# All complex products of the S5 tables on VectorE, both parts added in one step, and priority for the q, k and v projections

## The chip, the cores and the metric
The kernel runs on one core of one Trainium2 chip. A time is the device time of one execution in microseconds (us); lower is better. The engines are called as the profile calls them: PE is TensorE, PEld its weight loads, DVE is VectorE, ACT is ScalarE, POOL is GpSimd, SP issues most DMAs.

## The reference, cut to what matters
One encoder layer over 512 tokens of width 1024 in float32: a normalised input is projected into u, q, k, v, z and gates; an S5 mixer (a diagonal complex state space, forward and backward) works on u, a gated delta rule on q, k, v; then cross-attention over a memory of 256 rows, and a mixture of 32 experts, two for each token.
```
u, q, k, v, z, beta_f, beta_b, a_f, a_b = _split_cols(h @ w_in[l])
...
lam_bar = jnp.exp(lam * step)
b_bar = ((lam_bar - 1.0) / lam)[:, :, None] * b
...
_, h = lax.associative_scan(combine, (a, bu), reverse=reverse, axis=1)
return (jnp.einsum('bsgp,gcp->bsgc', h.real, c_re.astype(F32))
        - jnp.einsum('bsgp,gcp->bsgc', h.imag, c_im.astype(F32)))
...
qkv = jax.nn.silu(_centred_depthwise_conv(jnp.concatenate([q, k, v], axis=-1), conv_w))
...
u_c = lax.linalg.triangular_solve(l_mat, v_beta, left_side=True, lower=True, unit_diagonal=True)
```

## The kernel before, in words
The S5 scan is done in blocks of eight tokens. For it `s5_params` builds tables of powers of the complex decay times b and c: for each of eight rounds gg it makes two complex products of 128 partitions x 512 elements, **pm** (powers aF times b1) and **ca** (powers aR times ct). `cmul` makes a complex product of six instructions (four multiplications, a subtraction, an addition), on VectorE or on GpSimd by the two tables CA_ENG and PM_ENG (1 is GpSimd): nine of the sixteen products on GpSimd, seven on VectorE. The tensor engine then transposes pm (L372), an ACT copy takes it to bcT, `s5_u` multiplies it with u into U (L404), and ca is multiplied with bb into the table wl (L381).

In the same stretch stand the twelve projections of q, k and v (four heads each). `gdn_in` takes one after the other: `proj` is eight matmuls 128x512 with K = 1024 (L143; each matmul leaves two records in the trace), then a depthwise convolution of four scalar_tensor_tensor instructions on VectorE (L639), SiLU on ACT, transposes on PE (L648), and a norm. `weave((qkv, 13), (s5, 9))` writes the two streams' instructions alternately. Each engine's order is fixed before the run by the scheduler of the tile framework: an instruction's place in the code is its priority, unless a priority block raises it, and the scheduler lets what it takes to be ready earlier go first.

The stages behind it, by the names that the argument uses. **The gates**: small matmuls of the gates into a bank, gc copied from it on VectorE (L579), exponentials on ACT (L580, L583), and copies (L589 to L598). **The inversion** (`gdn_inv`): four rounds, each with an outer difference on PE (L703), e on VectorE (L707), exponentials on ACT, products of k with k and q (L716, L717) and N on VectorE (L720); then a transpose NT (L731), 31 substitution steps on VectorE, transposes XT and XN (L749, L750), and small matmuls (L768 to L778). It is woven with the four z projections (32 matmuls of the L143 kind), with key and value blocks of the memory (`mem_kv`, eight matmuls 128x256 each at L143 and two transposes at L958) and with the 62 steps of the S5 recurrence on VectorE (four instructions 128x64, L414 to L417). **The chain** (`gdn_chain`): eight chunks x four heads, L834 (products with the state), L835 (r, on VectorE), L840 (a product that this text counts from 1 to 32), L851 and L854 (the new state), woven with the remaining key and value blocks. After it come the S5 output (`s5_out`, L446), the mixing, the cross-attention, and the experts, whose weights stream from HBM (L1340).

Of the kernel before, what the change touches and what calls it, by code (L numbers as in the profile page):

```python
# [9 lines left out]
F32 = mybir.dt.float32  # L10
# [4 lines left out]
AF = mybir.ActivationFunctionType  # L15
OP = mybir.AluOpType
# [15 lines left out]
P = 128  # L32
# [11 lines left out]
def weave(*streams):  # L44

    live = [[g, n, 0] for g, n in streams]
    while live:
        s = min(live, key=lambda t: (t[2] + 0.5) / t[1])
        s[2] += 1
        if next(s[0], s) is s:  # L50
            live.remove(s)


CA_ENG = (1, 1, 0, 1, 1, 1, 0, 1)
PM_ENG = (0, 0, 1, 0, 1, 0, 1, 0)


class Enc:
# [162 lines left out]
    def cmul(self, eng, pool, ore, oim, are, aim, bre, bim, shape, tag):  # L221
# [7 lines left out]
        eng.tensor_tensor(oim, aim, bre, op=OP.mult)  # L229
        eng.tensor_tensor(oim, oim, t2, op=OP.add)  # L230

    def s5_params(self):
        nc, A, tc = self.nc, self.A, self.tc
        sp = self.s5p
        v, g_ = nc.vector, nc.gpsimd
        with tc.tile_pool(name="s5t", bufs=1, side="right") as tq:
            ct = tq.tile([P, 2, 32, 16], F32, name="ct")
            dT = tq.tile([16, 32], F32, name="dT")
            aF = tq.tile([P, 2, 8, 32], F32, name="aF")
            aR = tq.tile([P, 2, 8, 32], F32, name="aR")  # L240
            bb = tq.tile([P, 2, 34, 16], F32, name="bb")
            b1 = tq.tile([P, 2, 32, 16], F32, name="b1")
            with tc.tile_pool(name="s5i", bufs=1, side="right") as tp:
                lamrow = tp.tile([32, 2, 128], F32, name="lamrow")
                for di, dn in enumerate('fb'):
# [18 lines left out]
                ps = self.ps("s5")  # L264
# [7 lines left out]
                for ri in range(2):  # L272
                    ps = self.ps("s5")
                    for b in range(4):
                        nc.tensor.transpose(ps[:, b * P:(b + 1) * P], crow[:, ri, b, :], self.ident)
                    nc.scalar.activation(ct[:, ri].rearrange("p g c -> p (g c)"), ps, AF.Copy, scale=1.0 - 2.0 * ri)

                tl = lambda s: tp.tile([P, 32], F32, name="q" + s)
                step, mg, th, r, sn, cs, t1, t2 = (tl(s) for s in ("st", "mg", "th", "r", "sn", "cs", "t1", "t2"))
# [18 lines left out]
                pw = tp.tile([P, 2, 9, 32], F32, name="pw")  # L298
# [41 lines left out]
                v.memset(bb[:, :, 32:34], 0.0)  # L340
                bg = lambda ap: ap[:, :, None].to_broadcast([P, 32, 16])
                self.cmul(v, tp, bb[:, 0, :32], bb[:, 1, :32], bg(fre), bg(fim), bt[:, 0], bt[:, 1], [32, 16], "d")
                self.cmul(v, tp, b1[:, 0], b1[:, 1], bg(pw[:, 0, 1]), bg(pw[:, 1, 1]), bb[:, 0, :32], bb[:, 1, :32], [32, 16], "d")
            yield
            with tc.tile_pool(name="s5l", bufs=1, side="right") as tl:

                dd = tl.tile([P, 8, 16], F32, name="dd")
                v.memset(dd, 0.0)
                for cg in range(4):
                    v.tensor_tensor(dd[cg * 32:cg * 32 + 16], self.ident[:16, None, :16].to_broadcast([16, 8, 16]),  # L350
                                    dT[:, cg * 8:(cg + 1) * 8, None].to_broadcast([16, 8, 16]), op=OP.mult)
                for gg in range(8):
                    gs = slice(gg, 32, 8)
                    shp = [4, 8, 16]
                    am = lambda a, ri: a[:, ri, :, gs].rearrange("p m g -> p g m")[:, :, :, None].to_broadcast([P] + shp)
                    bm = lambda b, ri: b[:, ri, gs, None, :].to_broadcast([P] + shp)

                    pm = tl.tile([P, 2] + shp, F32, name="pm", bufs=1)
                    e = PM_ENG[gg]
                    self.cmul((v, g_)[e], tl, pm[:, 0], pm[:, 1], am(aF, 0), am(aF, 1), bm(b1, 0), bm(b1, 1), shp, f"P{1 - e}")  # L360

                    ca = tl.tile([P, 2] + shp, F32, name="ca", bufs=1)
                    e = CA_ENG[gg]
                    self.cmul((v, g_)[e], tl, ca[:, 0], ca[:, 1], am(aR, 0), am(aR, 1),
                              bm(ct, 0), bm(ct, 1), shp, f"P{1 - e}")
                    nc.sync.dma_start(self.ca_scr[gg], ca.rearrange("p r g m c -> p (r g m c)"))

                    bcT = tl.tile([P, 4, 2, P], F32, name="bct", bufs=1)
                    for ri in range(2):
                        ps = self.ps("s5")  # L370
                        for cg in range(4):
                            nc.tensor.transpose(ps[:, cg * P:(cg + 1) * P], pm[:, ri, cg].rearrange("p m c -> p (m c)"), self.ident)  # L372
                        nc.scalar.activation(bcT[:, :, ri, :], ps.rearrange("p (g q) -> p g q", g=4), AF.Copy)
                    self.s5_u(gg, bcT)

                    pd = [self.ps("s5") for _ in range(2)]
                    for cg in range(4):
                        g = cg * 8 + gg
                        for di in range(2):
                            for ri in range(2):  # L380
                                nc.tensor.matmul(pd[di][cg * 32:cg * 32 + 32, :128],  # L381
                                                 bb[di * 64:(di + 1) * 64, ri, g:g + 2].rearrange("p g c -> p (g c)"),
                                                 ca[di * 64:(di + 1) * 64, ri, cg].rearrange("p m c -> p (m c)"),
                                                 start=(ri == 0), stop=(ri == 1))
                    wl = tl.tile([P, 15, 16], F32, name="wl", bufs=2)
                    pv = [t[:, :128].rearrange("p (m c) -> p m c", c=16) for t in pd]
                    v.tensor_copy(wl[:, 0:8], pv[1])
                    v.tensor_copy(wl[:, 8:15], pv[0][:, 1:8])
                    v.tensor_tensor(wl[:, 7], wl[:, 7], pv[0][:, 0], op=OP.add)
                    v.tensor_tensor(wl[:, 7], wl[:, 7], dd[:, gg], op=OP.add)  # L390
                    for cg in range(4):
                        nc.sync.dma_start(self.w_scr[:, gg * 4 + cg],
                                          wl[cg * 32:cg * 32 + 16].rearrange("p e c -> p (e c)"))
                    yield
# [1112 lines left out]
    def build(self):  # L1507
        nc, tc, ctx, A = self.nc, self.tc, self.ctx, self.A
# [18 lines left out]
        pool = lambda st, name, **kw: st.enter_context(tc.tile_pool(name=name, bufs=1, **kw))  # L1527
# [21 lines left out]
        with tc.tile_pool(name="gi", bufs=2) as gi:  # L1549
            qkv = self.gdn_in([(w, n, h) for h in range(4) for w, n in ((1, "k"), (0, "q"))] +  # L1550
                              [(2, "v", h) for h in range(4)], gi)
            s5 = self.s5_params()
            next(s5)
            for _ in u:
                pass
            weave((qkv, 13), (s5, 9))

        self.gp2 = pool(left, "gp2")
        self.gp3 = pool(left, "gp3")
# [112 lines left out]
        with tc.tile_pool(name="wk", bufs=2, **rt) as wk, tc.manual_schedule(engines={mybir.EngineType.PE, mybir.EngineType.SP}):  # L1672
# [44 lines left out]
            for b in range(4):  # L1717
                t = tile_at(b, "yb")
# [59 lines left out]
```

## Time and profile before
| what | value |
|---|---|
| runs | 889.67, 893.03, 893.8 us; median 893.03 us |
| the profiled execution | 892.26 us, span 890.5 us |
| mean granted clock of PE (1 is full) | 0.948 |
| busy: PE, PEld | 783.1 us (88%), 492.2 us (55%) |
| busy: DVE, ACT, POOL | 404.3 us (45%), 329.4 us (37%), 232.6 us (26%) |

Times are those of the slowest core; here there is one. Shares are of the whole span; the stage that the change touches is read by itself in the rows below.

### The profile page before, as it was taken

The page shows a single profiled execution, that of the slowest core. Times are in us where ns is not written, and L with a number is a line of the kernel's source. Part 1 is how long each engine was busy: PE and PEld are TensorE (multiplying, and loading weights), DVE is VectorE, ACT ScalarE, POOL GpSimd, SP SyncE. Part 2 cuts the span into 40 slices and gives each one's busy share as a digit, 9 for nine tenths or more (in the row PEclk, how much of TensorE's full clock was granted, in tenths as well). Part 3 has the DMA queues.
Part 4 walks back from the last instruction along what each step waited for, and adds up shares of the span by engine and source line. Part 5 has one row for each costly group of instructions (what it writes and reads, how often), then busy time and mean ns, then how long its engine had stood idle before and what let it go on. Part 6 is the DMA issues. An engine that isn't in the chain of part 4 may idle for free. (4 is left out here: it accounts for less than half of the span.)

```text
span 890.5 us, 12981 instructions
## 1 busy us (share of the span) xinstructions
PE 783.1 (88%) x4735; PEld 492.2 (55%) x4736; DVE 404.3 (45%) x1044; ACT 329.4 (37%) x760; POOL 232.6 (26%) x237
## 2 busy tenths in 40 slices
PE   5986998998997997899899999996698878788983
PEld 3443554555586875676688879895333333333331
DVE  4288767678899522244643554324210000000375
ACT  4242454455413235465343464333232131312204
POOL 1022857832100111205161332241311011100103
PEclk9996998999997998999999999998799999999997
DMA  7837222322663308615663714595699999999982
GB/s 206 144 91 111 74 78 74 100 76 98 225 193 104 108 24 169 116 56 172 184 224 96 260 49 159 194 406 187 248 391 412 414 411 408 395 391 410 410 350 102
DMA packets 128130, 185.17 MB, mean 208 GB/s; under 512 B 38734, under 2 KB 93006, under 8 KB 123968
## 3 DMA queue, kind: packets, MB, share of 16 engines
q1 hardware_dynamic: 122736, 172.31, 57.6%
q0 software_dynamic: 5328, 12.01, 3.6%
q8 instruction: 38, 0.62, 0.3%
q14 instruction: 28, 0.23, 0.1%
HBM read 165.50 MB, written 26.18 MB: 215 GB/s over the span
## 5 line engine op out<-in xcount | busy, mean ns | idle before, releaser
L143 PE MATMUL bank<-ht,wst 128*128 128x512 f32 x320 | 151.3, 621 | 4.2 <-ACT kd L583 2.4
L1340 PE MATMUL bank<-mw,xt 128*64 128x512 f32 x360 | 104.5, 595 | 1.5 <-DMA mw<-in_moe_w_up_dram 1.5
L143 PEld LDWEIGHTS bank<-ht,wst 128*128 128x128 f32 x320 | 60.7, 198 | 73.4 <-issue 68.3
L1344 DVE SCALAR_TENSOR_TENSOR hs<-hs,tw,bank 128x256 f32<-128x256 f32 x16 | 7.7, 480 | 168.9 <-ACT hs L1343 168.9
L1343 ACT ACTIVATE hs<-bank,tw 128x256 f32<-128x256 f32 x16 | 7.6, 474 | 155.5 <-PE bank L1340 155.5
L1380 PE MATMUL bank<-mw,hT 128*64 128x512 f32 x152 | 50.6, 660 | 16.2 <-ACT yd L1385 16.2
L1340 PEld LDWEIGHTS bank<-mw,xt 128*64 128x64 f32 x360 | 33.5, 138 | 55.6 <-issue 52.4
L143 PE MATMUL bank<-mt,wst 128*128 128x256 f32 x256 | 59.9, 393 | 0.0
L639 DVE SCALAR_TENSOR_TENSOR cv<-xp,taps,cv 128x512 f32<-128x512 f32 x48 | 50.4, 1049 | 20.8 <-ACT cv L637 19.7
L972 POOL TENSOR_TENSOR wlo<-wst,whi 128x1024 fp32r<-128x1024 f32 x16 | 38.6, 2416 | 78.7 <-ACT whi L971 78.7
L143 PEld LDWEIGHTS bank<-mt,wst 128*128 128x128 f32 x256 | 50.0, 198 | 7.7 <-issue 0.6
L1320 POOL DMA_INDIRECT xg<-t_scr,tidx x16 | 16.5, 1029 | 136.4 <-PE bank L1327 133.4
L824 POOL TENSOR_TENSOR kt<-kn,kd 64x512 f32<-64x512 f32 x14 | 14.5, 1035 | 97.6 <-PE bank L778 49.8
L1330 ACT ACTIVATE xt<-bank,gm 128x128 f32<-128x128 f32 x128 | 34.7, 382 | 8.9 <-PE bank L1327 7.8
L149 PE MATMUL bank<-wlo,oh 128*128 128x256 f32 x128 | 36.6, 289 | 0.0
L854 DVE SCALAR_TENSOR_TENSOR S<-S,egl,bank 128x128 f32<-128x128 f32 x48 | 15.5, 345 | 46.1 <-PE bank L851 46.1
L150 PE MATMUL bank<-whi,oh 128*128 128x256 f32 x128 | 35.8, 283 | 0.0
L1380 PEld LDWEIGHTS bank<-mw,hT 128*64 128x64 f32 x152 | 14.0, 148 | 38.7 <-issue 20.8
L151 PE MATMUL bank<-whi,ol 128*128 128x256 f32 x128 | 35.3, 287 | 0.0
L149 PE MATMUL bank<-mlo,mxh 128*128 128x512 f32 x64 | 25.8, 405 | 0.8 <-DVE gss L484 0.8
L903 POOL TENSOR_TENSOR mlo<-mst,mhi 128x512 fp32r<-128x512 f32 x16 | 22.0, 1393 | 14.8 <-ACT mhi L902 14.2
L150 PE MATMUL bank<-mhi,mxh 128*128 128x512 f32 x64 | 25.7, 402 | 0.0
(551 smaller groups left out, 1826.3 us busy)
## 6 DMA issues: line engine op xcount, KB each, us to landing
mw<-in_moe_w_down_dram SPq DMA_DIRECT2D x23, 1024.0 KB, 14.7
mw<-in_moe_w_gate_dram SPq DMA_DIRECT2D x45, 512.0 KB, 8.3
mw<-in_moe_w_up_dram SPq DMA_DIRECT2D x45, 512.0 KB, 13.9
wst<-in_w_in_dram SPq DMA_DIRECT2D x20, 512.0 KB, 4.5
ca_scr<-ca SPq DMA_DIRECT2D x8, 512.0 KB, 2.7
wst<-in_xa_wk_dram SPq DMA_DIRECT2D x8, 512.0 KB, 4.3
y_scr<-lhc SPq DMA_DIRECT2D x2, 2048.0 KB
wst<-in_xa_wv_dram SPq DMA_DIRECT2D x8, 512.0 KB, 4.3
```

What stands on the lines that cost most here:

```text
L143: self.nc.tensor.matmul(ps, w[:, k, :], act[:, k, :], start=(k == 0), stop=(k == 7))
L149: self.nc.tensor.matmul(ps, ah, bl, start=(first and i == 0), stop=False)
L150: self.nc.tensor.matmul(ps, ah, bh, start=False, stop=False)
L151: self.nc.tensor.matmul(ps, al, bh, start=False, stop=(last and i == n - 1))
L639: v.scalar_tensor_tensor(cv, xp[:, w:w + T], taps[:, w, m:m + 1], cv, op0=OP.mult, op1=OP.add)
L854: v.scalar_tensor_tensor(sn, S[di, h], self.egl[:, ch % 2, ch // 2, di * 4 + h:di * 4 + h + 1], p, op0=OP.mult, op1=OP.add)
L903: nc.gpsimd.tensor_tensor(lo[:, k], st, hi[:, k].bitcast(F32), op=OP.subtract)
L972: nc.gpsimd.tensor_tensor(lo, st, hi.bitcast(F32), op=OP.subtract)
L1320: self.gather = g_.indirect_dma_start(out=xg, out_offset=None, in_=self.t_scr, in_offset=bass.IndirectOffsetOnAxis(ap=self.tidx[:, q:q + 1 ...
L1330: nc.scalar.activation(xt[:, k], ps[:, (k % 4) * P:(k % 4 + 1) * P], AF.Copy, scale=self.gm[:, k:k + 1])
L1340: nc.tensor.matmul(pg[w * 64:w * 64 + 64].rearrange("p (a n) -> p a n", a=2), xt[:, k, w * 64:w * 64 + 64], un[k // 4 * 2 + w][:, :, k % 4 ...
L1380: nc.tensor.matmul(py[w * 64:w * 64 + 64], hT[:, k, w * 64:w * 64 + 64], wd[w][:, k, c], start=(k == 0), stop=(k == 1))
```

## The change
There are no tables of engines any more: all sixteen products run on VectorE, by `cprod`. It takes four multiplications of 128x512, two of them into a tile cpt that holds both parts, and one addition of 128x1024 over both parts, five instructions for six. So that the real part is an addition too, ct and b1 have a third slice with a negated imaginary part, made by one more ACT copy each. All products share the one cpt. The convolution instructions and the sizes of all else are unchanged. Besides, the generator of the q, k and v projections is wrapped in `ahead`, which raises the priority of each of its steps.
```diff
@@ -51,8 +51,15 @@
-CA_ENG = (1, 1, 0, 1, 1, 1, 0, 1)
-PM_ENG = (0, 0, 1, 0, 1, 0, 1, 0)
+def ahead(tc, g):
+
+    while True:
+        with tc.high_priority():
+            if next(g, g) is g:
+                return
+        yield
...
@@ -229,17 +236,26 @@
+    def cprod(self, pool, o, am, a, bm, b):
+
+        v = self.nc.vector
+        t = pool.tile(list(o.shape), F32, name="cpt", bufs=1)
+        for ri in range(2):
+            v.tensor_tensor(o[:, ri], am(a, 0), bm(b, 1 + ri), op=OP.mult)
+            v.tensor_tensor(t[:, ri], am(a, 1), bm(b, ri), op=OP.mult)
+        v.tensor_tensor(o, o, t, op=OP.add)
...
-            ct = tq.tile([P, 2, 32, 16], F32, name="ct")
+            ct = tq.tile([P, 3, 32, 16], F32, name="ct")
...
-            b1 = tq.tile([P, 2, 32, 16], F32, name="b1")
+            b1 = tq.tile([P, 3, 32, 16], F32, name="b1")
...
-                    nc.scalar.activation(ct[:, ri].rearrange("p g c -> p (g c)"), ps, AF.Copy, scale=1.0 - 2.0 * ri)
+                    nc.scalar.activation(ct[:, 1 + ri].rearrange("p g c -> p (g c)"), ps, AF.Copy, scale=1.0 - 2.0 * ri)
+                nc.scalar.activation(ct[:, 0].rearrange("p g c -> p (g c)"), ps, AF.Copy)
...
-                self.cmul(v, tp, b1[:, 0], b1[:, 1], bg(pw[:, 0, 1]), bg(pw[:, 1, 1]), bb[:, 0, :32], bb[:, 1, :32], [32, 16], "d")
+                self.cmul(v, tp, b1[:, 1], b1[:, 2], bg(pw[:, 0, 1]), bg(pw[:, 1, 1]), bb[:, 0, :32], bb[:, 1, :32], [32, 16], "d")
+                nc.scalar.activation(b1[:, 0], b1[:, 2], AF.Copy, scale=-1.0)
...
                     pm = tl.tile([P, 2] + shp, F32, name="pm", bufs=1)
-                    e = PM_ENG[gg]
-                    self.cmul((v, g_)[e], tl, pm[:, 0], pm[:, 1], am(aF, 0), am(aF, 1), bm(b1, 0), bm(b1, 1), shp, f"P{1 - e}")
+                    self.cprod(tl, pm, am, aF, bm, b1)
 
                     ca = tl.tile([P, 2] + shp, F32, name="ca", bufs=1)
-                    e = CA_ENG[gg]
-                    self.cmul((v, g_)[e], tl, ca[:, 0], ca[:, 1], am(aR, 0), am(aR, 1),
-                              bm(ct, 0), bm(ct, 1), shp, f"P{1 - e}")
+                    self.cprod(tl, ca, am, aR, bm, ct)
...
@@ -1553,7 +1568,7 @@
-            weave((qkv, 13), (s5, 9))
+            weave((ahead(tc, qkv), 13), (s5, 9))
```

The instruction order changes on two engines in three places that matter below. Line numbers of the changed kernel are higher than those of before by 7 at L143, by 8 to 17 in the table code and by 15 from L404 on. First, VectorE from the end of b1 (b_392) to the first pm; bank_280 holds the gates' sums, and P_637 and P_638 are scratch tiles of cmul, as cpt is of cprod. Before:
```order
L579 COPY gc<-bank_280 128x32
L228 TENSOR_TENSOR b_392<-b_392,d_560 128x512
L230 TENSOR_TENSOR b_392<-b_392,d_561 128x512
L582 TENSOR_TENSOR sdl<-bank_280,gc 128x32
L589 SCALAR_TENSOR_TENSOR sbe<-beta,egc 128x16
L594 TENSOR_SCALAR csr<-egc 64x4x4
```
and, some rows on:
```order
L225 TENSOR_TENSOR P_637<-aF,b_392 128x512
L226 TENSOR_TENSOR P_638<-aF,b_392 128x512
L593 COPY csr<-sbe 64x4x4 x2
L227 TENSOR_TENSOR pm<-aF,b_392 128x512
L229 TENSOR_TENSOR pm<-aF,b_392 128x512
L350 TENSOR_TENSOR dd<-ident,dT 16x128 x4
L228 TENSOR_TENSOR pm<-pm,P_637 128x512
L230 TENSOR_TENSOR pm<-pm,P_638 128x512
```
After:
```order
L366 MEMSET dd 128x128
L244 TENSOR_TENSOR pm<-aF,b_392 128x512 x2
L245 TENSOR_TENSOR cpt<-aF,b_392 128x512
L244 TENSOR_TENSOR ca<-aR,ct 128x512
L368 TENSOR_TENSOR dd<-ident,dT 16x128 x4
L244 TENSOR_TENSOR ca<-aR,ct 128x512
L245 TENSOR_TENSOR cpt<-aF,b_392 128x512
L594 COPY gc<-bank_280 128x32
L246 TENSOR_TENSOR pm<-pm,cpt 128x1024
L597 TENSOR_TENSOR sdl<-bank_280,gc 128x32
```
The copy of gc stands ahead of the products before; it now stands behind the four multiplications of pm and two of ca's four, with only the addition of pm behind it. The ca product of this round was on GpSimd.

Second, PE at the end of the q, k, v stage. Bank numbers 1771, 1838, 1905 and 1976 of L150 are the four z projections; L387, L396 and L419 are the transposes of pm, the products of ca and the products into U of the last two rounds; L718 is the first instruction of the inversion. After:
```order
L150 MATMUL bank_1838<-ht,wst 128x512 x3
L150 MATMUL bank_1905<-ht,wst 128x512 x6
L387 MATMUL bank_1599<-ident,pm 128x128 x4
L387 MATMUL bank_1605<-ident,pm 128x128 x4
L150 MATMUL bank_1905<-ht,wst 128x512 x2
L396 MATMUL bank_1629<-ca,bb 32x128 x8
L150 MATMUL bank_1976<-ht,wst 128x512 x3
L419 MATMUL bank_1611<-uperm,bct 64x64 x16
L396 MATMUL bank_1630<-ca,bb 32x128 x8
L718 MATMUL bank_1720<-lef,g 64x64 x8
```
All but five of the 32 z matmuls now stand ahead of the inversion's first matmul. Before, the z projections stood between the inversion's four rounds, each as in this place (L703 and L716 belong to the inversion, L143 is z):
```order
L716 MATMUL bank_1838<-kT 64x64
L717 MATMUL bank_1838<-qT,kT 64x64
L716 MATMUL bank_1838<-kT 64x64
L717 MATMUL bank_1838<-qT,kT 64x64
L143 MATMUL bank_1868<-ht,wst 128x512 x8
L703 MATMUL bank_1884<-lef,g 64x64 x8
L703 MATMUL bank_1884<-geb,g 64x64 x8
L716 MATMUL bank_1905<-kT 64x64
```

Third, PE between the end of the substitution and the chain's first product. Before (mt,wst blocks are keys and values; L768, L776 and L778 the small inversion matmuls):
```order
L768 MATMUL bank_2210<-XT,N 32x32 x16
L768 MATMUL bank_2228<-XT,N 32x32 x16
L768 MATMUL bank_2246<-XT,N 32x32 x16
L958 MATMUL bank_2458<-ident,kvo 128x128 x2
L143 MATMUL bank_2532<-mt,wst 128x256 x8
L776 MATMUL bank_2282<-R,XN 32x32 x16
L778 MATMUL bank_2320<-XN,R 32x32 x16
L776 MATMUL bank_2358<-R,XN 32x32 x16
L778 MATMUL bank_2382<-XN,R 32x32 x16
L958 MATMUL bank_2545<-ident,kvo 128x128 x2
L143 MATMUL bank_2661<-mt,wst 128x256 x8
L840 MATMUL bank_2415<-vc,lhc 128x128
```
After:
```order
L150 MATMUL bank_2731<-mt,wst 128x256 x8
L783 MATMUL bank_2162<-XT,N 32x32 x16
L783 MATMUL bank_2180<-XT,N 32x32 x16
L783 MATMUL bank_2198<-XT,N 32x32 x16
L783 MATMUL bank_2216<-XT,N 32x32 x16
L791 MATMUL bank_2252<-R,XN 32x32 x16
L793 MATMUL bank_2290<-XN,R 32x32 x16
L791 MATMUL bank_2328<-R,XN 32x32 x16
L793 MATMUL bank_2352<-XN,R 32x32 x16
L973 MATMUL bank_2744<-ident,kvo 128x128 x2
L150 MATMUL bank_2831<-mt,wst 128x256 x8
L855 MATMUL bank_2385<-vc,lhc 128x128
```
Before, nine key and value blocks (the first at the end of the z projections, 2047) stand ahead of L768, one stands among the small matmuls and one behind them; now twelve stand ahead of the same place (L783), none among them and one behind. So five blocks before, and three after, are left behind the first chain product (L840, L855). On VectorE, 11 recurrence steps instead of 23 stand ahead of the transpose NT, 33 instead of 44 ahead of XT, 39 ahead of the chain's last inversion copies (L801), and 54 instead of 62 ahead of the first r.

## Rows read from the trace of the kernel before

**Rows 1.** Windows: us; PE, PEld, DVE, ACT, POOL busy; PEclk; DMA share; GB/s
```profile
62.66:202.50 139.84, 126.72 (x838) 67.61 (x838) 103.29 (x152) 60.49 (x170) 81.64 (x86) 0.93 0.35 85
```

**Rows 2.** PE timeline: start, us, line, tiles, count [idle before <-what ended it]
```profile
62.66 1.98 PE L143 MATMUL bank<-ht,wst 128*128 128x512 f32 x4 [2.35 <-ACT kd L583]
...
74.84 1.94 PE L372 MATMUL bank<-ident,pm 128*128 128x128 f32 x8 [7.39 <-DVE pm L228]
...
102.32 8.75 PE L143 MATMUL bank<-ht,wst 128*128 128x512 f32 x20
...
143.72 0.63 PE L381 MATMUL bank<-ca,bb 64*32 64x128 f32 x2 [4.03 <-POOL xp L634]
...
144.28 7.44 PE L143 MATMUL bank<-ht,wst 128*128 128x512 f32 x10
```

**Rows 3.** Windows: two short stretches, columns as in rows 1
```profile
72.00:84.00 12.00, 9.16 (x33) 4.95 (x34) 11.84 (x20) 1.97 (x4) 1.66 (x4) 0.50 0.70 117
...
145.00:149.00 4.00, 4.00 (x6) 1.64 (x5) 3.77 (x5) 2.65 (x12) 4.00 (x4) 0.50 0.33 131
```

**Rows 4.** DVE timeline at the first table and inside the stage
```profile
59.90 0.18 DVE L579 COPY gc<-bank 128x32 f32<-128x32 f32 x1
...
60.60 0.68 DVE L230 TENSOR_TENSOR b<-b,d 128x512 f32<-128x512 f32 x1
...
68.44 1.75 DVE L229 TENSOR_TENSOR pm<-aF,b 128x512 f32<-128x512 f32 x1
...
113.93 3.11 DVE L639 SCALAR_TENSOR_TENSOR cv<-xp,taps,cv 128x512 f32<-128x512 f32 x4 [3.38 <-ACT cv L637]
...
116.96 0.68 DVE L227 TENSOR_TENSOR pm<-aF,b 128x512 f32<-128x512 f32 x1
117.56 0.68 DVE L229 TENSOR_TENSOR pm<-aF,b 128x512 f32<-128x512 f32 x1
...
136.28 6.26 DVE L639 SCALAR_TENSOR_TENSOR cv<-xp,taps,cv 128x512 f32<-128x512 f32 x4 [2.49 <-ACT cv L637]
```

**Rows 5.** ACT timeline behind the gates
```profile
61.58 1.03 ACT L194 ACTIVATE ut<-bank 128x512 f32<-128x512 f32 x1
```

**Rows 6.** POOL timeline ahead of the wait at 143.72 us
```profile
141.96 1.71 POOL L228 TENSOR_TENSOR ca<-ca,P 128x512 f32<-128x512 f32 x1
...
143.62 0.09 POOL L633 MEMSET xp<- 128x2 f32 x1
```

**Rows 7.** DVE timeline of the inversion and of the first chain update
```profile
239.91 0.68 DVE L707 TENSOR_TENSOR e<-bank,gc 128x512 f32<-128x512 f32 x1
...
245.57 1.97 DVE L731 STREAM_TRANSPOSE NT<-N 128x1024 f32<-128x1024 f32 x1
...
280.43 2.03 DVE L750 STREAM_TRANSPOSE XN<-X 128x1024 f32<-128x1024 f32 x1
...
283.19 0.23 DVE L414 TENSOR_TENSOR rt<-a8r,U 128x64 f32<-128x64 f32 x1
...
284.10 0.23 DVE L414 TENSOR_TENSOR rt<-a8r,U 128x64 f32<-128x64 f32 x1
...
312.22 0.35 DVE L835 SCALAR_TENSOR_TENSOR r<-bank,csr,vc 128x128 f32<-128x128 f32 x1 [5.44 <-PE bank L834]
```

**Rows 8.** PE timeline from the inversion to the S5 output
```profile
287.91 4.69 PE L143 MATMUL bank<-mt,wst 128*128 128x256 f32 x16
...
301.82 0.38 PE L840 MATMUL bank<-vc,lhc 128*128 128x128 f32 x2
...
331.09 0.39 PE L840 MATMUL bank<-r,lhc 128*128 128x128 f32 x2
...
335.38 0.49 PE L840 MATMUL bank<-r,lhc 128*128 128x128 f32 x2
...
347.45 0.66 PE L446 MATMUL bank<-tz,uperm 128*64 128x128 f32 x2 [4.67 <-DMA tz<-w_scr]
```

**Rows 9.** The chain that ended last: start, duration, engine, tile
```profile
634.30 7.25 PE bank L1340 x32
...
641.91 9.67 DMA mw<-in_moe_w_up_dram
```

## Prediction
> **What bounds the kernel now.** The table beside the span says that PE is busy for 88% and VectorE for 45% of the whole, but the change touches one stage, so I read the windows view for that stage alone, from the first q, k, v matmul to the first matmul of the inversion. There PE is busy for 126.7 of 139.8 us at a granted clock of 0.93, VectorE for 103.3, GpSimd for 81.6 [rows 1]. PE has idle time of 139.8 − 126.7 = 13.1 us in it, and the timeline says where: 7.4 us before the transposes of the first pm, 4.0 us before a product of ca, the rest in small pieces [rows 2]. The 2.35 us on the first of these rows lie just ahead of the window. In between PE goes from one projection to the next: ten matmuls (20 records) in 8.75 us, 0.875 us each, none waiting [rows 2]. After each of the two long waits the granted clock is 0.50, the lower of PE's two levels (1.2 against 2.4 GHz) [rows 3]; the ten records at 144.28 took 7.44 us where ten of the fast row take 4.4 [rows 2].
>
> The third view is VectorE's timeline. The same kind of 128x512 product took 1.75 us at 68.44 and 0.60 us (start to start) at 116.96; four convolution steps took 3.1 us at 113.93 and 6.3 us at 136.28 [rows 4]. At 141.96 GpSimd is at a complex product of its own, 1.71 us for one of six instructions, and the memset that the next convolution needs is queued behind it [rows 6]; that row is where PE's 4.0 us go. So in this stage PE sets the time, and the waits that it has are waits for tables made by two engines that run at once.
>
> Behind the stage, the chain that ended last goes through PE (7.25 us of expert matmuls at 634.30) to a weight transfer that starts when PE frees its buffer [rows 9]: what PE gains ahead of the experts is carried to the end.
>
> **The change part by part.** *Price of a product.* No instruction of 128x1024 with two float32 operands of this kind is in the rows; it costs between one 512 step (0.60) and two (1.20). I take 1.15, near the two, since the 128x1024 transpose takes 1.97 and scales with its elements as far as the rows tell [rows 7]. A product is then 4 × 0.60 + 1.15 = 3.55 us, sixteen are 56.8. The seven before cost between 7 × 6 × 0.60 = 25 and 7 × 6 × 1.75 = 74 us; with the convolutions in their contended mix I put them at 37. Twelve convolutions at 3.03 are 36.4, and what remains of 103.3 is other small work, 16 us as an estimate. VectorE then has 57 + 36 + 16 ≈ 110 us to do, PE 126.7 less about 8 us of lost clock, 118, and 23.6 us of z matmuls that are moved in (27 × 0.875). PE has more; GpSimd's 54 product instructions are gone, and with them the 1.75 us rows.
>
> *Term 1, the first table.* Before, PE waits 2.35 + 7.39 = 9.7 us here [rows 2]. After, b1 is done at 61.3 (60.60 + 0.68) [rows 4]; then come a memset, 0.1, six multiplications at 0.60, four small dd steps, about 1.0, gc, 0.1, and the wide addition, 1.15: the pm is there at 61.3 + 5.9 = 67.2. PE ran out of work at 62.66 − 2.35 = 60.3, so it would wait 6.9. But gc now stands behind the products, at 66.0, and from gc (59.90) to the end of ut, the copy that frees what the next projection needs, 2.7 us pass [rows 4, 5]: 68.7, which costs some 0.5 more. Wait 7.4, gain 2.3 us. The lower clock behind it (0.50 from 72 to 84 [rows 3]) I take to stay.
>
> *Term 2, the rest of the stage.* There PE idles for 13.1 − 7.4 = 5.7 us and loses 7.4 − 4.4 = 3 us to the lower clock at 144.28 [rows 2]: 8.7. Each group now costs VectorE two products (7.1 us) and, by the group, one and a half convolutions (4.5), so about 11.6 with little else; PE has one and a half projections (10.5) and the small matmuls of the group in it. The cover is thin. With z matmuls ahead of the inversion PE has something to go on with, so I leave 2 us of waits: gain 6.7. At the last S5 product the kernel is 9.0 us ahead, were it not for z.
>
> *Term 3, the inversion's four rounds.* The z matmuls used to fill PE while VectorE and ACT made e and N. They now come first: the last S5 product ends at 202.5 − 9.0 + 23.6 = 217.1. Behind it stand a U copy of 128x512 (1.0, from the like copy [rows 5]), six recurrence steps at 0.91 (284.10 − 283.19 [rows 7]) and four rounds, of which the first two stand side by side: three times 5.66 (239.91 to 245.57 [rows 7]) is 17.0. With 1 us for the last products: 217.1 + 1.0 + 1.0 + 5.5 + 17.0 = 241.6 for NT, against 245.57. Only 4 of the 9 us are left. The other end: of the 43.1 us from 202.5 to NT before, the four z projections took 4 × 7.0 = 28.0; the 15.1 us that are left give 232.2, 13 ahead. I take the first value, since the recurrence steps, which lay under the z matmuls, now stand in the open.
>
> *Term 4, substitution to the first r.* The 36.9 us from NT to XN's end (282.46) stay [rows 7]. From there to the first chain product 19.4 us pass, with two key and value blocks; one is moved ahead of the substitution's end, where PE has nothing else, and one block took half of the 16 records and more, 4.69 us at the low clock of that place [rows 8]: 14.7 us, 293.3 for the first chain product, 8.5 ahead. The first r on VectorE has 15 recurrence steps (13.7 us) ahead of it behind the inversion's copies, so it is there at about 303.7 against 312.22 [rows 7]: 8.5 ahead too.
>
> *Term 5, blocks out of the chain.* From r at 312.22 to product 9 at 331.09 it takes 18.9 us [rows 7, 8] with blocks between the products; where none is between, two steps take 4.3 us (331.09 to 335.38), 2.15 each. Three blocks, no longer five, are in the chain, and all of them ahead of product 5; five steps of 2.15 make 10.8. Product 9 is 8.5 + 8.1 = 16.6 ahead. The S5 output begins at 347.45, 16.4 us behind product 9 [rows 8]; three steps of the chain that used to stand ahead of it are likely to come behind (it is released by the recurrence and a transfer, not by the chain), at 2.15 to 3.9 us each. Net 13 to 18; I take 15.
>
> Two ACT copies more (1.03 each by the like row [rows 5]) lie on ACT, busy for 60 of 140 us, and are costed at nothing; if they stood in front of pm they would cost 2 us.
>
> The sum against the profiled execution is 892.3 − 15 = 877.3; it lies 0.8 us below the median, so the median should be 893.0 − 15 = **878.0 us**, with 866 to 885 for this case by itself (term 3's other end, 9 us, and 3 of term 5 more; 4 of terms 1 and 2 and 3 of term 5 less).
>
> **A rule against it.** PE's busy share of 91% in the stage [rows 1] is the ground on which I call it the bound. The Trainium skill, Perfetto Trace Analysis, in the section Identifying the Most-Contended Engine, holds that a matmul's busy share is a poor measure of how near TensorE is to its limit, while for VectorE occupancy is the measure. By it VectorE's 74%, going to 110 of 140 us, would set the stage, and the time would be that of the first rival below. The row at 102.32, twenty records without a gap at 0.44 us a record, speaks for PE in the middle of the stage; the rule bears on its ends.
>
> **The rivals.** *VectorE becomes the bound (slower).* pm, ca and cpt have one buffer each, so products cannot run ahead of the transposes that read pm, and each group may make PE wait for VectorE. What speaks for it is the thin cover in term 2; what speaks against it are GpSimd's contended rows, which go. The point of decision is 15 / 8 = 1.9 us per group: from there the gain is gone. With a wait like the one at 143.72 (4.0 us) in each of the eight groups, 32 − 15 = 17 us are lost: 910. Chance 0.15. *The gain stays small.* Terms 1 to 4 hold, but the chain's steps are held by the latency from PE to VectorE and ACT and back, not by the blocks, so that only r's 8.5 us, or a little less, are left: 886. Chance 0.17. *A wash.* The z matmuls and waits of VectorE only change places, term 3 eats all of the 9 us, and nothing later is earlier: 893. Chance 0.12.
>
> **How the numbers follow.** The forecast has 0.56. Half a per cent, 4.5 us, is about what a measurement of this kernel tells from no change. The forecast and nearly all of the small gain are faster, 0.71; the wash and the edge of the small gain are the same, 0.14; the first rival is slower, 0.15. The range takes in the forecast, the small gain and the wash and leaves the slower rival out: 864 (866 and the 2 us of waits left in term 2) to 894.
>
> **What would show it.** Right: no 128x512 row on VectorE over 1 us in the stage; PE's wait for the first pm near 7 us and none over 2 us in the later groups; the last S5 product near 217; NT near 242; the first chain product near 293; the first r near 304; the S5 output some 15 us earlier. Wrong: waits of PE for pm, cv or U with VectorE as what ends them in each group, or NT later than 246 us.

## The result and the profile after

The changed kernel takes 880.77 us (median of 4; 875.45 to 885.02), the kernel before 891.75 us over its 4 executions. The ratio is 0.9874, 95% interval 0.9839 to 0.9909: faster by 11.0 us. Medians here and below are of all executions, while ratios and intervals compare with the kernel before taken beside that run and leave out executions over 1.5% above the fastest of their kernel, so where the two differ the ratio decides. The forecast was 878.0 us, range 864 to 894. The profiled execution has a span of 878.0 us, 12.5 less than before.

The windows view of the stage, from the first whole q, k, v block to the inversion, answers to [rows 1] (columns as there):
```profile
61.69:213.50 151.81, 146.03 (x906) 78.17 (x904) 106.70 (x196) 69.39 (x184) 20.54 (x33) 0.98 0.43 115
```
The stage is longer because 27 z matmuls are in it now. PE is idle for 5.8 us of it (13.1 before), the granted clock is 0.98 (0.93), and GpSimd's 82 us are down to 21. VectorE has 107 us in 152. PE's timeline, as in [rows 2]:
```profile
61.69 1.88 PE L150 MATMUL bank<-ht,wst 128*128 128x512 f32 x4
64.05 0.49 PE L132 MATMUL bank<-ident,U 128*128 128x128 f32 x2 [0.48 <-ACT mt L138]
69.47 1.94 PE L387 MATMUL bank<-ident,pm 128*128 128x128 f32 x8 [4.93 <-issue]
71.63 8.04 PE L150 MATMUL bank<-ht,wst 128*128 128x512 f32 x16
...
138.70 0.63 PE L387 MATMUL bank<-ident,pm 128*128 128x128 f32 x4 [0.30 <-DVE wl L404]
...
212.90 0.66 PE L396 MATMUL bank<-ca,bb 64*32 64x128 f32 x16
```
There is one wait for the first pm (5.4 us in two pieces, 9.7 before), then a single one of 0.30 us up to the last S5 product at 213.6. No group makes PE wait. The profile names nothing that ends the 4.93 us ("issue"), but the wide addition that finishes pm stands on VectorE up to 69.36:
```profile
68.14 1.22 DVE L246 TENSOR_TENSOR pm<-pm,cpt 128x1024 f32<-128x1024 f32 x1
```
The low clock behind the first wait is short, 6.7 us in the windows view against 12 in [rows 3]; eight matmuls take 8.04 us at 71.63 where the stage has 7.03:
```profile
67.00:73.70 6.70, 4.23 (x13) 3.19 (x14) 6.25 (x19) 5.07 (x10) 0.20 (x4) 0.50 0.11 42
```

VectorE's groups by line from 56 to 225 us, before and then after (mean ns behind the comma); the count of 48 is that of the twelve convolutions:
```profile
L639 DVE SCALAR_TENSOR_TENSOR cv<-xp,taps,cv 128x512 f32<-128x512 f32 x48 | 50.4, 1049 | 20.8 <-ACT cv L637 19.7
L229 DVE TENSOR_TENSOR pm<-aF,b 128x512 f32<-128x512 f32 x5 | 5.5, 1110 | 0.0
```
```profile
L654 DVE SCALAR_TENSOR_TENSOR cv<-xp,taps,cv 128x512 f32<-128x512 f32 x48 | 35.5, 746 | 1.3 <-DVE cv L654 0.5 <-ACT cv L652 0.2
L244 DVE TENSOR_TENSOR pm<-aF,b 128x512 f32<-128x512 f32 x16 | 10.3, 682 | 4.3 <-PE bank L387 4.2
L246 DVE TENSOR_TENSOR pm<-pm,cpt 128x1024 f32<-128x1024 f32 x8 | 9.8, 1221 | 0.1
```
The rows that stood next to GpSimd's products are shorter: the product row from 1110 to 682 ns, and the convolution step from 1049 to 746 ns, which alone is 15 us of VectorE's time. The inversion and the chain, as in [rows 7, 8], from the timelines of VectorE and PE:
```profile
240.76 1.97 DVE L746 STREAM_TRANSPOSE NT<-N 128x1024 f32<-128x1024 f32 x1
275.79 2.00 DVE L765 STREAM_TRANSPOSE XN<-X 128x1024 f32<-128x1024 f32 x1
305.13 0.35 DVE L850 SCALAR_TENSOR_TENSOR r<-bank,csr,vc 128x128 f32<-128x128 f32 x1
```
```profile
293.96 0.38 PE L855 MATMUL bank<-vc,lhc 128*128 128x128 f32 x2
316.64 0.49 PE L855 MATMUL bank<-r,lhc 128*128 128x128 f32 x2
326.95 0.66 PE L461 MATMUL bank<-tz,uperm 128*64 128x128 f32 x2 [3.33 <-DMA tz<-w_scr]
```
NT is 4.8 us earlier, the first chain product 7.9, the first r 7.1, product 9 14.5, the S5 output 20.5. So far it reads as the forecast had it. The experiments show that this is only half of the story.

### The profile page after: what moved, and what is told of

Same layout as the page of the kernel before. It is cut to its first block, busy times and chain, and to the rows that moved or that the text cites. A ratio compares the mean times of both kernels' runs of the same rounds, so it can differ in the third digit from the quotient of the medians.

```text
span 878.0 us, 12960 instructions
## 1 busy us (share of the span) xinstructions
PE 778.2 (89%) x4735; PEld 491.0 (56%) x4736; DVE 398.7 (45%) x1082; ACT 328.3 (37%) x759; POOL 164.8 (19%) x183
## 5 line engine op out<-in xcount | busy, mean ns | idle before, releaser
L150 PE MATMUL bank<-ht,wst 128*128 128x512 f32 x320 | 146.5, 608 | 1.4 <-ACT ut L201 1.4
L150 PEld LDWEIGHTS bank<-ht,wst 128*128 128x128 f32 x320 | 60.1, 195 | 69.8 <-issue 67.2
L150 PE MATMUL bank<-mt,wst 128*128 128x256 f32 x256 | 58.7, 387 | 0.0
L150 PEld LDWEIGHTS bank<-mt,wst 128*128 128x128 f32 x256 | 49.2, 195 | 7.3 <-issue 0.7
L654 DVE SCALAR_TENSOR_TENSOR cv<-xp,taps,cv 128x512 f32<-128x512 f32 x48 | 35.5, 746 | 1.3 <-DVE cv L654 0.5
L918 POOL TENSOR_TENSOR mlo<-mst,mhi 128x512 fp32r<-128x512 f32 x16 | 21.4, 1357 | 40.6 <-ACT mhi L917 21.8
L839 POOL TENSOR_TENSOR kt<-kn,kd 64x512 f32<-64x512 f32 x14 | 14.5, 1037 | 76.9 <-PE bank L793 46.7
L681 POOL TENSOR_TENSOR rs<-ss,nhalf 128x4 f32<-128x4 f32 x8 | 15.5, 1936 | 65.3 <-DVE ss L680 35.1
## 6 DMA issues: line engine op xcount, KB each, us to landing
y_scr<-lhc SPq DMA_DIRECT2D x2, 2048.0 KB, 11.3
```

Of the source, the lines that this page charges most:

```text
L150: self.nc.tensor.matmul(ps, w[:, k, :], act[:, k, :], start=(k == 0), stop=(k == 7))
L654: v.scalar_tensor_tensor(cv, xp[:, w:w + T], taps[:, w, m:m + 1], cv, op0=OP.mult, op1=OP.add)
L681: g_.tensor_tensor(rs, ss, self.nhalf[:, :4], op=OP.pow)
L918: nc.gpsimd.tensor_tensor(lo[:, k], st, hi[:, k].bitcast(F32), op=OP.subtract)
```

## The experiments

Theory A, that of the prediction: PE's waits came from tables made by two engines at once; putting all products on VectorE takes them away, and the new order adds a part of its own. Rivals: B, the order alone does it; C, the wide addition is needed. The first four kernels take the parts of the change one by one.

**Priority alone**
```diff
...
-            weave((qkv, 13), (s5, 9))
+            weave((ahead(tc, qkv), 13), (s5, 9))
```


> Kernel before plus the priority for q, k, v alone; nine of sixteen products stay on GpSimd. In its instruction order 27 of 32 z matmuls stand ahead of the inversion and 11 of 16 key and value blocks ahead of L768 (12 in the changed kernel, 9 before). Theory A (the waits for tables made by two engines are what went, the new order is a second, smaller part): VectorE's 128x512 rows stay at 1.1 to 1.75 us next to GpSimd, some PE waits over 2 us stay in the stage, and half of the gain at most is there: 885 to 890 us. Theory B (the order alone made it, the engine of the products is of no account): the whole gain, 879 to 883 us.


Measured: 886.16 us, ratio 0.9924 (0.9897 to 0.9952). As A has it: the convolution step stays at 1050 ns (x48), and PE waits for 13.1 us for the first pm. The order alone is worth 6.7 us by the ratio (4.3 between the profiled spans).

**The products alone** (the changed kernel without the priority)
```diff
-            weave((ahead(tc, qkv), 13), (s5, 9))
+            weave((qkv, 13), (s5, 9))
```


> The changed kernel without the priority. 8 more z matmuls than before stand ahead of the inversion, and the key and value blocks stand as before (9 ahead of L768, the last behind chain product 8). Theory A: the waits in the table stage go (terms 1 and 2, 9 us, of which term 3 takes some 2), term 5 is absent: 884 to 887 us. Theory B: no change, 889 to 893 us.


Measured: 893.35 us, ratio 1.0017 (0.9988 to 1.0046). The total is what B expects, but the rows contradict B: NT stands at 224.3, the first chain product at 279.9 and the S5 output at 327.8 us, about 20 us ahead of before [rows 7, 8]. The gain is there at 328 us and gone at 424, where the chain's last product stands (before: 417).

**Six instructions, all on VectorE**, no priority
```diff
-CA_ENG = (1, 1, 0, 1, 1, 1, 0, 1)
-PM_ENG = (0, 0, 1, 0, 1, 0, 1, 0)
+CA_ENG = (0,) * 8
+PM_ENG = (0,) * 8
```


> Kernel before with both engine tables set to VectorE: all sixteen products there, by the old six instructions, no priority. 16 x 6 x 0.60 = 57.6 us of VectorE against 56.8 by the wide addition, so by theory A it is like the run with the products alone within 2 us: 884 to 889 us. Theory C (the addition of both parts in one step is needed, as it frees VectorE or shortens each table): no gain, 890 us or more.


Measured: 868.92 us, ratio 0.9742 (0.9699 to 0.9785). C falls, and A undersized it: two lines of the kernel before, with neither of the change's other parts, gain 22 us, twice what the change does. In the windows view its stage is all PE:
```profile
62.00:180.40 118.40, 116.92 (x838) 64.40 (x836) 99.97 (x195) 61.03 (x170) 11.87 (x32) 0.99 0.41 100
```
The same 838 records as in [rows 1] took 118 us where they took 140. The rows ahead of the first pm show how. VectorE's timeline there, before and then in this kernel:
```profile
62.72 1.07 DVE L597 COPY cso<-egc 64x16 f32<-64x16 f32 x1
70.11 3.86 DVE L350 TENSOR_TENSOR dd<-ident,dT 16x128 f32<-16x128 f32 x4
```
```profile
60.88 0.16 DVE L597 COPY cso<-egc 64x16 f32<-64x16 f32 x1
65.75 1.16 DVE L350 TENSOR_TENSOR dd<-ident,dT 16x128 f32<-16x128 f32 x4
```
Before, GpSimd was at products of its own beside both rows. From the end of b1 to the end of the first pm VectorE took 14.0 us, here 8.0, and PE's wait of 7.39 us for that pm is gone.

**Six instructions on VectorE, with the priority** (both diffs above)


> All sixteen products on VectorE by six instructions, with the priority. Its order has 14 z matmuls ahead of the inversion and the key and value blocks as before (last behind chain product 8), unlike the changed kernel. Theory A: the table stage as in the changed kernel, term 5 absent: 884 to 888 us. Theory B: the priority is there, 879 to 883 us. Theory C: 890 us or more.


Measured: 899.25 us, ratio 1.0087 (1.0057 to 1.0118). A and B miss; the time lies where C has it (890 or more), but C had fallen with the run before, so none of the three explains it.

So parts do not add up: with six instructions the priority costs 30 us, with five it gains 13. To see where, I summed two things over windows of 4 us in each profiled execution: PE's idle time, and busy time x (1 − granted clock), the time that the lower clock cost. Each cell is idle + clock in us; "sum" is up to 460 us, less that of before, and stands beside the change of the span.

| kernel | 0 to 56 | 56 to 320 | 320 to 460 | sum | span |
|---|---|---|---|---|---|
| before | 11.6 + 0.0 | 24.0 + 16.1 | 12.2 + 5.4 | | 890.5 |
| changed | 13.9 + 1.4 | 13.4 + 8.8 | 13.5 + 5.5 | −12.8 | −12.5 |
| priority alone | 11.5 + 0.0 | 21.4 + 13.9 | 9.1 + 7.5 | −5.9 | −4.3 |
| products alone | 13.0 + 1.8 | 12.2 + 7.1 | 9.2 + 26.9 | +0.9 | +1.2 |
| six on VectorE | 10.1 + 0.0 | 13.2 + 7.8 | 9.5 + 4.6 | −24.1 | −23.2 |
| six with priority | 10.8 + 0.0 | 16.0 + 9.1 | 9.8 + 21.1 | −2.5 | +0.3 |

The sums follow the spans within 3 us. All kernels with the products on VectorE have some 15 to 21 us less in the middle column. The two that lose it again do so in the third column, and by the clock, not by idle time. The windows view of the products-alone kernel there:
```profile
392.00:420.00 28.00, 28.00 (x113) 21.08 (x112) 7.29 (x13) 5.56 (x12) 6.21 (x6) 0.53 0.20 65
```
PE is busy without a gap for 28 us at the lower level. Its timeline shows where that begins:
```profile
392.04 0.43 PE L817 MATMUL bank<-vn,qkd 64*64 64x128 f32 x2
392.39 1.05 PE L498 MATMUL bank<-ones,s5q 128*128 128x1 f32 x8
393.38 0.45 PE L817 MATMUL bank<-vn,qkd 64*64 64x128 f32 x2
393.64 0.60 PE L818 MATMUL bank<-vn,qkd 64*64 64x128 f32 x2
394.05 0.63 PE L817 MATMUL bank<-vn,qkd 64*64 64x128 f32 x2
```
Eight records of 128x1 (the column sums of squares of the S5 gate), then the chain's output products, which go from 0.43 us a pair to 0.63. The next kernel changes these 128x1 matmuls alone.

**Wide column sums in the products-alone kernel**
```diff
+        onesw = sp.tile([P, P], F32, name="onesw")
+        nc.vector.memset(onesw, 1.0)
...
-                nc.tensor.matmul(ps[:, b:b + 1], sq[:, b * P:(b + 1) * P], self.ones, start=True, stop=True)
-            nc.vector.tensor_copy(ss[:, m], ps[:, 0:4])
+                nc.tensor.matmul(ps[:, b * P:(b + 1) * P], sq[:, b * P:(b + 1) * P], onesw, start=True, stop=True)
+            nc.vector.tensor_copy(ss[:, m], ps.rearrange("p (b f) -> p b f", b=4)[:, :, 0])
```


> The run with the products alone (no priority), with one difference: the 16 column sums of squares of the S5 gate are taken against 128 columns of ones instead of one, so that eight records of 128x1 in a row become eight of 128x128. The instruction order of every engine is otherwise the same. In the products-alone run PE was busy without a gap from 392 to 420 us at a granted clock of 0.50, beginning behind such a group of eight. Theory L (the 20 us that the products gain are lost again in that low-clock stretch, which the thin group sets off): the clock stays at 1.00 there, about 14 of the 28 us come back, 872 to 880 us. Rival M (the loss is in the chain's order, and the clock has nothing to do with it, or falls in any case): 889 to 895 us.


Measured: 883.79 us, ratio 0.9919 (0.9890 to 0.9949), against 1.0017 without. The same window and place:
```profile
392.00:420.00 28.00, 24.99 (x166) 18.26 (x162) 14.52 (x31) 11.39 (x21) 8.96 (x14) 1.00 0.44 145
```
```profile
392.52 1.16 PE L500 MATMUL bank<-onesw,s5q 128*128 128x128 f32 x8
393.61 0.43 PE L819 MATMUL bank<-vn,qkd 64*64 64x128 f32 x2
393.88 0.38 PE L820 MATMUL bank<-vn,qkd 64*64 64x128 f32 x2
```
The order is the same and the group takes no more time than its thin form (1.16 against 1.05), yet the clock stays at 1.00 and the chain's last product comes at 411 instead of 424 us. Theory L is shown in its mechanism. Its size is short: 9.6 us came back (8.7 by the ratios), not 14 or more; in the wide kernel the lower level came at 421 to 431 us, behind a real gap of PE of 2.9 us.

**The same in the changed kernel** (control)


> Control: the changed kernel with the same wide column sums. Its clock stayed at 1.00 among these matmuls, so by theory L there is nothing to give back: 878 to 883 us, as the changed kernel. If the wide sums were good for time by themselves, it would gain as much as the products-alone run does.


Measured: 883.48 us, ratio 0.9916 (0.9890 to 0.9941): no gain, as expected where the clock had not fallen (the median is half a microsecond above the range). The order of PE, VectorE and ACT around the column sums is not quite the changed kernel's (from 387 us on), so the control with six instructions below, whose order there is its partner's, is the stronger one. With the thin group out of play, the five-instruction kernel is as fast without the priority (0.9919) as with it.

**The negated ct on GpSimd**, in the changed kernel. The second thing that the table shows is the first column: the changed kernel and the products-alone kernel lose 3 to 4 us against before ahead of 56 us, and 5 against six on VectorE. ACT's timeline there, in the changed kernel:
```profile
42.65 0.62 ACT L292 ACTIVATE ct<-bank 128x512 f32<-128x512 f32 x1
43.16 0.59 ACT L293 ACTIVATE ct<-bank 128x512 f32<-128x512 f32 x1
...
44.00 1.28 ACT L311 ACT_TABLE_LOAD   x1
45.30 0.23 ACT L311 ACTIVATE qsn<-qr 128x32 f32<-128x32 f32 x1
45.43 0.21 ACT L312 ACTIVATE qt<-qr 128x32 f32<-128x32 f32 x1
45.66 1.28 ACT L571 ACT_TABLE_LOAD   x1
46.96 0.23 ACT L571 ACTIVATE se<-sa 128x32 f32<-128x32 f32 x1
47.20 1.28 ACT L313 ACT_TABLE_LOAD   x1
48.50 0.32 ACT L313 ACTIVATE qcs<-qt,halfpi 128x32 f32<-128x32 f32 x1
48.84 1.28 ACT L573 ACT_TABLE_LOAD   x1
```
The new copy (L293) moved se between the sine and the cosine, so that ACT loads a table four times instead of twice. Before, se stood ahead of both, and the only loads were:
```profile
45.04 1.28 ACT L294 ACT_TABLE_LOAD   x1
47.05 1.28 ACT L558 ACT_TABLE_LOAD   x1
```
```diff
-                nc.scalar.activation(ct[:, 0].rearrange("p g c -> p (g c)"), ps, AF.Copy)
+                g_.tensor_scalar(ct[:, 0].rearrange("p g c -> p (g c)"), ct[:, 2].rearrange("p g c -> p (g c)"), -1.0, None, op0=OP.mult)
```


> The changed kernel with the negated third slice of ct made on GpSimd from the second one, instead of by an ACT copy. In the changed kernel ACT's order at 43 to 50 us has four table loads of 1.28 us where the six-instruction kernel has two, and aF is ready 2.8 us later; with this edit ACT's order there is that of before again. Theory N (the extra ACT copy costs two table loads, on the path to the first table): the gates' matmul at about 49 us instead of 51.7, the first pm some 3 us earlier; 875 to 879 us if nothing behind it moves. Rival: the extra copy is hidden, 880 to 882 us. The order behind it changes too (14 z matmuls fewer ahead of the inversion, two key and value blocks fewer ahead of L768), so the rows of the start count, the total less.


Measured: 878.68 us, ratio 0.9859 (0.9831 to 0.9887). ACT has two table loads there again, and on PE's timeline the gates' matmuls and the first pm are 3.3 us earlier:
```profile
48.41 0.36 PE L589 MATMUL bank<-g,lef 128*128 128x16 f32 x2 [0.26 <-DVE qfi L352]
...
66.14 1.94 PE L387 MATMUL bank<-ident,pm 128*128 128x128 f32 x8 [4.93 <-issue]
```
The rows of the start are as theory N has them. Of the total only 2 us are seen, within the intervals of the two.

**The same without the priority**


> The same edit without the priority: five instructions, all on VectorE, no extra ACT copy of ct. Its order is near that of the products-alone run (last key and value block behind chain product 8). If the wide addition itself is good, the table stage is as fast as with six instructions (inversion begins at 188 us with 136 matmuls ahead of it, 180 with 128). The total hangs on the low-clock stretch by theory L: 868 to 872 us if the clock stays up behind 390 us, 885 to 892 us if it falls again.


Measured: 890.99 us, ratio 0.9976 (0.9945 to 1.0008). The clock fell again (0.50 from 389 to 417 us), and the total is the one expected for that. The table stage is as fast as with six instructions: the inversion begins at 186.1 us, 188 expected.

**Six on VectorE, with an idle load on GpSimd.** Is it the slow tables or the contention that the move takes away? This kernel does all products on VectorE and beside them, in place of the old nine, 54 products on GpSimd whose results nobody reads.
```diff
...
+    def gload(self, pool, a, b, shape):
+        g = self.nc.gpsimd
+        t = pool.tile([P] + shape, F32, name="gl", bufs=1)
+        u = pool.tile([P] + shape, F32, name="gm", bufs=1)
+        for _ in range(3):
+            g.tensor_tensor(t, a, b, op=OP.mult)
+            g.tensor_tensor(u, a, b, op=OP.mult)
...
+                    if PM_OLD[gg]:
+                        self.gload(tl, am(aF, 0), bm(b1, 0), shp)
...
```


> The kernel with all sixteen products on VectorE by six instructions (868.9 us), and beside each of the nine products that were on GpSimd before, six multiplications of the same operands on GpSimd into tiles that nobody reads (54 in all, so the work of the engine is as before while no table waits for it). The order on PE, VectorE and ACT differs in two to four places only. Theory K (what the move takes away is the contention: VectorE's convolution steps take 1049 ns next to GpSimd's products and 747 without): the convolution rows go back to about 1.0 us, VectorE becomes late, half or more of the 22 us is lost: 878 to 888 us. Rival (what the move takes away is the wait for slow tables, 6 x 1.1 to 1.7 us each on GpSimd): no table waits for GpSimd here, so 868 to 873 us, even with slower rows on VectorE.


Measured: 905.32 us, ratio 1.0191 (1.0148 to 1.0234). Theory K, beyond its range: 36 us are lost against the same kernel without the load. Its stage in the windows view, and two groups of VectorE from 56 to 225 us:
```profile
62.00:215.20 153.20, 126.31 (x836) 68.47 (x834) 143.47 (x198) 60.38 (x169) 85.92 (x84) 0.89 0.31 76
```
```profile
L653 DVE SCALAR_TENSOR_TENSOR cv<-xp,taps,cv 128x512 f32<-128x512 f32 x48 | 44.8, 936 | 1.5 <-ACT cv L651 0.6
L231 DVE TENSOR_TENSOR ca<-aR,ct 128x512 f32<-128x512 f32 x8 | 9.1, 1135 | 0.0
```
VectorE is busy for 143 of 153 us and is the bound; PE idles for 27. The same instructions took 100 us without GpSimd beside them. The Trainium skill, SBUF — State Buffer, section Who interferes with whom, says that a VectorE instruction with two inputs in SBUF contends with a GpSimd instruction that reads SBUF, and that one of the two then blocks. The trace agrees: 684 ns alone, 1135 ns beside GpSimd for the ca product, the slowest of the product rows (one kept 683). The run shows what contention can cost when all sixteen products are on VectorE and no table waits for GpSimd. It does not divide the 22 us of the kernel before, which had seven products on VectorE: there the wait for the first pm came from stretched rows, as shown above, but the wait of 4.03 us ended with a memset queued behind GpSimd's product [rows 2, 6], which is a wait in that engine's queue.

**No priority, negated ct on GpSimd, wide column sums** (the three edits above)


> Five instructions on VectorE, no priority, the negated ct on GpSimd and the wide column sums; the order of the engines is that of the run without the wide sums (891 us), which had a granted clock of 0.50 from 389 to 415 us with PE busy. Theory L: the clock stays up there, 12 us come back: 877 to 881 us. Rival: 889 us or more.


Measured: 880.73 us, ratio 0.9887 (0.9845 to 0.9930); the chain's last product stands at 406 instead of 420 us. Theory L a second time; 7.9 us came back by the ratios.

**Six on VectorE with wide column sums**


> Control and the best version so far: six instructions on VectorE, no priority, wide column sums. In the run without them (868.9 us) the clock did not fall at that place, so by theory L nothing comes back: 867 to 871 us.


Measured: 868.96 us, ratio 0.9764 (0.9739 to 0.9790): nothing, as expected.

**Six on VectorE with the priority and wide column sums**


> Six instructions on VectorE with the priority and the wide column sums (without these: 899 us, with a granted clock of 0.50 from 400 to 413 us). Theory L: the clock stays up there, 7 to 10 us come back: 888 to 892 us in the same measure. What is then left over the six-instruction kernel without priority (868.9) is the price of the priority with these products; if the priority is harmless: 872 us or less.


Measured: 895.75 us, ratio 1.0017 (0.9986 to 1.0049), executions from 884 to 901. By the ratios 6.2 us of the expected 7 to 10 came back (3.5 by the medians). In the profiled execution, at 886 one of the shortest, the clock stays up from 400 to 413 us and the sum of the three columns is 13.5 us over that of the run above, without the priority: 4.2 in 56 to 320 and 10.3 in 320 to 460, less 1.0 ahead of 56. The price of the priority with six instructions is 18.5 us between the two profiled spans and 22.5 by the ratios; I can place three quarters of the former.

## Why the prediction was right

The time, the sign and the steps held; the account of where the gain is from was only partly right. That the time came out within 3 us is in part luck: term 2 is too small, and losses that the sum does not have (the reordered ACT, longer rounds, the tail) take about as much away.

- **What bounds.** Right: PE set the stage, VectorE did not become the bound with 107 of 152 us. The first rival is no idle one, though: with GpSimd's load beside it VectorE does become the bound. What kept it from that is the contention that went, as the forecast argued.
- **Price of a product.** Right: the wide addition takes 1.15 us start to start (68.14 to 69.29 us), the products 0.60. The reason given for it was no reason: both transposes of [rows 7] have 1024 columns, so they do not show that the time scales with the elements.
- **Term 1.** The wait for the first pm was forecast at 7.4 us and is 5.4, but not because pm came early: it is done at 69.4, where 67.2 was forecast. "Two ACT copies more ... are costed at nothing; if they stood in front of pm they would cost 2 us" failed: one copy reordered ACT, and its table loads make b1 end at 63.0 instead of 61.3. They also made PE itself late: it waits for the gates for 3.42 us at 51.73 and runs the next projection at a lower clock (8.81 us, 7.11 with the negated ct on GpSimd), so it runs out of work at 63.6, where the forecast had 60.3. With the negated ct on GpSimd the wait is 7.1 us, near the forecast.
- **Term 2.** Mis-sized. "I leave 2 us of waits", and 5 us at the low clock kept: 0.3 and 2.1 are left. Terms 1 and 2 made 9.0 us; the inversion's first matmul at 213.5, less 23.6 of z, is 12.6 ahead of before (202.5, which the forecast calls the last S5 product). The kernel with six instructions on VectorE reaches 22, so the true size of the waits and the lower clock is near all of the idle and clock time in the stage.
- **Term 3.** Right in kind: the z matmuls taken out of the rounds leave them in the open. The rounds take 27.2 us from the last S5 product to NT, 24.5 forecast; NT stood at 240.8 (241.6).
- **Term 4.** Right: first chain product 293.96 (293.3), first r 305.1 (303.7).
- **Term 5.** Product 9 is 14.5 us ahead (16.6 forecast), the S5 output 20.5 (23 to 28 by the term's own sum, though the list of signs says 15), and the router's first step 14.9 (616.4 to 601.4), where 15 was the net. But the chain is no shorter: from its first product to its last it takes 115.1 us, 115.2 before, so its last product is only 7.9 us ahead, as the rival of the small gain had it. The rest of the 14.9 lies beside the chain; the S5 output is a candidate that no run takes by itself.
- **The tail.** "What PE gains ahead of the experts is carried to the end": not whole. Of the 14.9 us, 13.9 are left at the last weight transfer (848.3 to 834.4) and 12.5 at the end.
- **What the forecast did not see.** It read the moved z matmuls and key and value blocks as a gain of terms 4 and 5. The six-instruction kernel keeps the old order there (first chain product to last: 115.5 us) and is 23 us earlier throughout, so the larger gain is VectorE's, free of GpSimd. The order is worth something alone (the first experiment), but the two do not add. By the table the changed kernel is 11.3 us behind the six-instruction one: 5.2 ahead of 56 us, 1.2 up to 320, 4.9 behind it. The first of these goes with the reordered ACT, whose removal brings the first pm 3.3 us forward but the total only 2. For the others no run decides. The z matmuls moved from under the rounds are a candidate (term 3: 43.1 to 27.2 us for 23.6 us of matmuls fewer, nearly 8 us in the open); against it stands the five-instruction kernel without priority, which moves only eight of them and is behind as well.

Open: why the priority costs so much more with six instructions than with five once the clock is up, why the five-instruction kernel without priority (880.7) stays 12 us behind the six-instruction one (both with wide column sums), of which the three columns place 7, and the spread of some kernels' executions (876 to 892 for the former), of which only one execution each was profiled.

## What to carry to other kernels

Before two-input elementwise work is shared between VectorE and GpSimd, compare the same VectorE row with and without GpSimd beside it: here the helper slowed the helped by 40%, and taking it away in two lines was worth twice the whole change. A new instruction is costed with the order that it brings about (an ACT copy of 0.6 us cost two table loads), and an edit to the order is judged by idle time and granted clock over all later stages, since it can set off a loss hundreds of microseconds further on.

## What was unexpected of the hardware

The lower clock came with PE busy in every microsecond: 28.00 of 28.00 us at 0.53, begun behind eight records of 128x1 and kept through small products of 64 rows; with 128 columns in place of one, in the same order, it did not come. The Trainium skill, TensorE: Matmul & The Clock Gate, section HAM oscillation — how this bites in real kernels, gives as its rule to leave no long idle gaps on PE; the trace shows a fall that such a rule does not cover. In all three pairs of kernels the clock fell within 2 us of the start of such a group in the thin form, without a gap of PE in the 10 us ahead, and not in the wide form. The group alone is not enough: in the six-instruction kernel four groups of 128x1 pass between 391 and 422 us with no fall. What the products behind the group add to it was not tried by itself.
